# Even layer of a two-layer backbone: where the modulation's row sums stand among the first projection blocks, and how many buffers the heads' results have

## The chip, the cores and the metric

One core of a Trainium2 chip runs the whole kernel in one launch. The metric is the device time of that launch in microseconds, the median of several executions. A profile is one profiled execution; its times are counted from the start of its span.

## The reference, cut to what matters

```python
def adaln(cond, w, b):
    m = jax.nn.silu(cond) @ w + b
    return jnp.split(m, 3, axis=-1)              # shift, scale, gate

def even_layer(x, ctx, c, c_ctx, ...):           # x 512x2048, ctx 256x2048
    sh, sc, gt = adaln(c, ada_w, ada_b)
    csh, csc, cgt = adaln(c_ctx, ada_w, ada_b)
    h  = modulate(rms_norm(x, norm_g), sh, sc)
    hc = modulate(rms_norm(ctx, norm_g), csh, csc)
    kc_t, vc_t = split(hc @ w_in[:, K and V])
    au, av, ag, bq, bk, bv, bg = split(h @ w_in)
    q, k = diff_qk(bq, qnorm_g, cos, sin), diff_qk(bk, knorm_g, cos, sin)
    ...                                          # attention over latents and context,
    return x + gt * (y @ w_out)                  # gated mixing, output projection

def odd_layer(x, c, ...):                        # a convolution module with its own adaln
    sh, sc, gt = adaln(c, ada_w, ada_b)
    h = modulate(rms_norm(x, norm_g), sh, sc)
    return x + gt * (conv_module(h, ...) @ w_out)
```

`diff_qk` normalises each head's 64 values and rotates them by position (the latents only). All is fp32. What the change moves is a part of `adaln`: the products of silu(c) with the gate part of the even layer's modulation weights and with the three parts of the odd layer's, four vectors of 2048.

## The kernel before

**Arithmetic.** Every fp32 matrix product is made of three: each operand is split into a high part (a cast to float32r) and a low part (the rest), and TensorE (PE) multiplies high by high, low by high and high by low. `load_w` (L98) does this for a granule of weights, four k-tiles of 128x512: a DMA of 1 MB in SP's queue into a `raw` buffer (three of them, shared with the row loads below), the high cast on ACT (L103), the subtraction on VectorE (DVE, L104). There are two buffers for each half.

**Blocks.** `m_block` (L170) makes a block of 512 output columns: one PSUM tile for each 128 tokens, six with the context and four without, from a ring of six (tag "m" of `psA`), and four granules. In each granule PE goes through the token tiles, 12 matmuls for each; a call `hook(gi)` follows each granule in the program. A latent tile uses `hhi` and `hlo`, a context tile the two halves of `hc`.

**The order of the work around the change.** First come the shift and scale of the even layer, interleaved with the first K block (L376 to L419). There PE's and SP's order is written out by hand; it fills `k0ps`, the tiles mb_333 to mb_338. Its last two context k-tiles end it: `make_hc` (L363 to L371) has PE transpose ctx (L366), ACT scale it into `hcf` (L368), and DVE make `hc`, high (L109) and low (L112). Then follow, in the program: `k_done(k0ps)`, the first V block (L593, tiles mb_1441 to mb_1446), `v_done`, some small loads (`rows2` and four `dwr`, L597 to L616, and lam), the second K block, the second V block, two Q blocks (L637, four tiles each), and from there AV, U, the attention and the output projection. A list scheduler decides how the engines' instructions stand against each other, outside the part written by hand: by its own simulation of the times, with weights preferred (`high_priority`). The order on each engine is fixed before the run.

**A K or Q result.** `qk_post` (L532) takes each finished tile: ACT squares it (L534), DVE reduces it (L537) and scales (L193), POOL takes the power -1/2 (L194, `rs`), DVE makes `tn` = tile times `rs` (L541), the last to read the PSUM tile, so that the tile is free for the next block, then for a latent tile the rotation (L549 to L555), for a context tile one product (L557). PE transposes the result `rot` (L560), ACT casts the high part (`qkhi`, L111), DVE subtracts (`qklo`, L112), and both are written to DRAM (L565). `qkhi` and `qklo`, and `vhi` and `vlo` of `v_post`, share a ring with the tag "hl" of three buffers; a buffer is free when its write to DRAM has landed.

**The row sums.** The four vectors of the modulation above are made beside the blocks. `ada_jobs` (L447) lists 64 rows, 16 for each vector: row jt is 128 lines of the weight matrix, 128x2048, 1 MB. `ada_add` (L464, L466) multiplies it by a column of silu(c) and adds it to `acc` on DVE; after 16 rows a tail sums over the partitions and writes it out (`spread`, `columns`, `row`, in later calls). A call of `ada_step` adds first the row loaded ahead, then takes and adds n rows from the `raw` ring, and with a pool `w0` loads one more ahead into w0's single buffer. So `hook0` (L590) adds two rows a call, `hook` one, and no call of theirs goes across the end of a vector. Before, `hook0` stands behind all granules of V, K, V and of Q's first block, `hook` behind those of Q's second.

Of the kernel before, what the change touches and what calls it, by code (L numbers as in the profile page):

```python
# [11 lines left out]
F32 = mybir.dt.float32  # L12
F32R = mybir.dt.float32r
# [6 lines left out]
P = 128  # L20
D = 2048
KT = D // P
T = 512
# [12 lines left out]
C_U, C_AV, C_AG, C_Q, C_K, C_BV, C_BG = 0, 1024, 2048, 3072, 4096, 5120, 6144  # L36
# [9 lines left out]
def hybrid_layers_kernel(  # L46
# [10 lines left out]
    e_ada_w, e_w_in, e_w_out = e_ada_w[0], e_w_in[0], e_w_out[0]  # L57
# [4 lines left out]
    def nm(s):  # L62
        uid[0] += 1
        return f"{s}_{uid[0]}"
# [187 lines left out]
    PE.transpose(tpz, rows1, ident[:96, :96])  # L252
    V.tensor_copy(g1, tpz)

    S = rp.tile([P, KT, 32], F32, name="S")
    V.memset(S, 0.0)
    th = tp.tile([P, 2 * KT], F32, tag="small", name="th")
    A.activation(th, g1[:, cC : cC + 2 * KT], AF.Tanh, scale=0.5)
# [59 lines left out]
    diag = tp.tile([P, T], F32, tag="a", name="diagx")  # L318
    rbz = zt()
    spread_cols(rbz, rsx, diag)  # L320
    rb = tp.tile([P, T], F32, tag="hl", bufs=3, name="rb")
    V.tensor_copy(rb, rbz)

    def load_ctx():
# [150 lines left out]
    def ada_step(zalloc, n=1, pool=None):  # L475
        if ada_tail:
            f = ada_tail.pop(0)
            f(zalloc)
            if f.__name__ == "spread":
                return  # L480
        done = False
        if ada_state["ahead"]:
            done = ada_add(ada_state["ahead"])
            ada_state["ahead"] = None
        for _ in range(n):
            if done or not (job := ada_take()):
                return
            done = ada_add(job)
        if pool and not done:
            ada_state["ahead"] = ada_take(pool)  # L490
# [41 lines left out]
    def qk_post(ps, which, tt, half, tok0, dst, rope):  # L532
        sq = tp.tile([P, 512], F32, tag="a", name=nm("sq"))
        A.activation(sq, ps, AF.Square)  # L534
        ms = tp.tile([P, 8], F32, tag="ms", bufs=4, name=nm("ms"))
        rs = tp.tile([P, 8], F32, tag="rs", bufs=4, name=nm("rs"))
        V.reduce_sum(ms, sq.rearrange("p (g d) -> p g d", d=DH), axis=AX.X)  # L537
        rstd_cols(rs, ms, 1.0 / DH, ms)
        tn = tp.tile([P, 512], F32, tag="b", name=nm("tn"))
        g3 = lambda a: a.rearrange("p (g d) -> p g d", d=DH)  # L540
        V.tensor_tensor(g3(tn), g3(ps), rs.unsqueeze(2).broadcast_to([P, 8, DH]), op=ALU.mult)  # L541
        r = tp.tile([P, 512], F32, tag="c", name=nm("rot"))
        if rope:
            CG, SG = CGs[which], SGs[which]
            g5 = lambda a: a.rearrange("p (g a b d) -> p (g a) b d", g=8, a=2, b=2)
            s5 = SG[:, tt, :].rearrange("p (a b d) -> p a b d", a=2, b=2)
            t5 = lambda a, b: a.rearrange("p (g a b d) -> p g a b d", g=8, a=2, b=2)[:, :, :, b, :]
            for b in range(2):
                V.tensor_tensor(  # L549
                    t5(r, b), t5(tn, 1 - b),  # L550
                    s5[:, :, b, :].unsqueeze(1).broadcast_to([P, 8, 2, 16]),
                    op=ALU.mult,
                )
            V.tensor_tensor(g3(tn), g3(tn), CG[:, tt, :].unsqueeze(1).broadcast_to([P, 8, DH]), op=ALU.mult)
            V.tensor_tensor(r, r, tn, op=ALU.add)  # L555
        else:
            V.tensor_tensor(g3(r), g3(tn), gains[which].unsqueeze(1).broadcast_to([P, 8, DH]), op=ALU.mult)  # L557
        z = zt()
        for i in range(4):
            PE.transpose(z[:, i * P : (i + 1) * P], r[:, i * P : (i + 1) * P], ident)  # L560
        hi = tp.tile([P, 4, P], F32R, tag="hl", bufs=3, name=nm("qkhi"))
        lo = tp.tile([P, 4, P], F32R, tag="hl", bufs=3, name=nm("qklo"))
        split(hi, lo, z.rearrange("p (a b) -> p a b", b=P))
        for s, tl in ((0, hi), (1, lo)):
            SP.dma_start(  # L565
                dst[4 * half : 4 * half + 4, s, :, tok0 : tok0 + P].rearrange("h p t -> p h t"), tl.bitcast(F32)
            )

    def v_post(ps, half, tok0):
        hi = tp.tile([P, 4, P], F32R, tag="hl", bufs=3, name=nm("vhi"))  # L570
        lo = tp.tile([P, 4, P], F32R, tag="hl", bufs=3, name=nm("vlo"))
        split(hi, lo, ps.rearrange("p (a b) -> p a b", b=P))
        for s, tl in ((0, hi), (1, lo)):
            SP.dma_start(
                v_s[4 * half : 4 * half + 4, s, tok0 : tok0 + P, :].rearrange("h t d -> t h d"), tl.bitcast(F32)
            )
# [5 lines left out]
    def v_done(ps, half):  # L582
        for b in range(NT + NTC):
            v_post(ps[b], half, b * P)
# [3 lines left out]
            qk_post(ps[b], 0, b, half, b * P, q_s, True)  # L588

    hook0 = lambda gi: ada_step(zt, 1, w0)  # L590
    hook, hook2 = (lambda gi, n=n: ada_step(zt, n) for n in (1, 2))
    k_done(k0ps, 0)
    ps = m_block(e_w_in, C_BV, both(), psA, "m", hook0)  # L593
    v_done(ps, 0)


# [36 lines left out]
    k_done(ps, 1)  # L633
    ps = m_block(e_w_in, C_BV + 512, both(), psA, "m", hook0)
    v_done(ps, 1)
    for hb in range(2):
        ps = m_block(e_w_in, C_Q + 512 * hb, lat(), psA, "m", hook if hb else hook0)  # L637
        q_done(ps, hb)
    p12a.close()

# [638 lines left out]
```

## Time and profile before

| | |
|---|---|
| median of 3 runs | 1862.2 us (1861.59 to 1863.13) |
| the profiled execution's own time | 1862.0 us |
| its span | 1860.2 us |
| mean granted TensorE clock | 0.994 |
| busy of the span: PE, PEld, DVE, ACT, POOL | 97%, 79%, 60%, 30%, 24% |
| DMA | 327.34 MB, mean 176 GB/s |

PE is TensorE's matmul, PEld its weight load, SP the engine whose queue issues the DMAs. A row of a timeline gives the start in us, the duration of one instruction (or of a run of equal ones together), engine, line, operation, what it writes and reads, and in brackets the idle time before it with what ended it. Matmuls are pipelined, so that a matmul's duration of 0.39 us is longer than the step to the next. A row of a window gives start and end, the length, then for PE, PEld, DVE, ACT and POOL the busy time with the count of instructions, PE's granted clock (1.00 is full), the mean busy share of the 16 DMA engines, and GB/s. In names the numbers are dropped by the profile; lists of the order keep them.

### The profile page before, as it was taken

How to read it: one execution, taken by the hardware profiler on the slowest of the kernel's cores; microseconds unless marked ns; L12 is line 12 of the kernel's file. 1: busy time of each engine (PE TensorE's matmuls, PEld its weight loads, DVE VectorE, ACT ScalarE, POOL GpSimd, SP SyncE). 2: the span in 40 equal slices, each digit the busy share in tenths (PEclk: the TensorE clock that was granted, in tenths of full speed). 3: DMA queues.
4: the chain of work that ended last, by engine and by line, in shares of the span. 5: the costliest groups of instructions: out<-in, count | busy, mean ns of one | idle time of the engine just before them, and what ended most of it. 6: DMA issues, size and time to landing. Idle time of an engine off the chain costs nothing.

```text
span 1860.2 us, 21958 instructions
## 1 busy us (share of the span) xinstructions
PE 1808.0 (97%) x8767; PEld 1478.0 (79%) x8767; DVE 1122.4 (60%) x1571; ACT 560.5 (30%) x747; POOL 451.2 (24%) x173
## 2 busy tenths in 40 slices
PE   5998999999999989999999999999999999999998
PEld 2556878888888878888888889888888888888887
DVE  4439545377656336667674555249999999765111
ACT  3322112122323134444442225322222222464120
POOL 0002002002000032323220002234544544444332
PEclk9998999999999999999999999999999999999999
DMA  9997763496667485565757663232233223224441
GB/s 321 359 347 243 246 201 115 145 348 227 207 246 248 150 224 165 159 193 149 213 184 241 237 223 106 76 106 91 91 108 97 91 93 112 91 91 141 145 159 53
DMA packets 208487, 327.34 MB, mean 176 GB/s; under 512 B 10249, under 2 KB 116610, under 8 KB 200194
## 3 DMA queue, kind: packets, MB, share of 16 engines
q1 hardware_dynamic: 208386, 325.94, 54.5%
q8 instruction: 69, 1.13, 0.3%
q14 instruction: 32, 0.26, 0.0%
HBM read 292.33 MB, written 33.58 MB: 175 GB/s over the span
## 4 chain that ended last, share of the span: by engine, by line
PE 81%; DMA 9%; DVE 4%; issue 3%; POOL 1%; ACT 1%; SPq 1%; DVEq 0%; ACTq 0%; POOLq 0%
PE tg L67 30%; PE mb L67 19%; PE m L67 14%; PE fm L67 8%; DMA raw<-in_o_ada_w_dram 2%; PE S L67 2%; PE z L305 2%; DMA raw<-in_e_ada_w_dram 2%; PE oT L67 2%; DVE wlo L104 1%; DVE acc L466 1%; DMA v_s<-vhi 1%; PE t L875 1%; DMA x<-in_x_dram 1%; DMA kk<-k_s 1%
## 5 line engine op out<-in xcount | busy, mean ns | idle before, releaser
L104 POOL TENSOR_TENSOR wlo<-raw,whi 128x2048 fp32r<-128x2048 f32 x80 | 369.5, 4619 | 636.7 <-ACT whi L103 629.3
L103 ACT CAST whi<-raw 128x2048 fp32r<-128x2048 f32 x136 | 259.9, 1911 | 686.9 <-PE tg L67 212.5
L1144 DVE SCALAR_TENSOR_TENSOR z<-y,dwc,z 128x512 f32<-128x512 f32 x480 | 319.2, 744 | 0.1
L67 PE MATMUL tg<-h2h,wlo 128*128 128x512 f32 x704 | 274.7, 390 | 0.0
L67 PE MATMUL tg<-h2l,whi 128*128 128x512 f32 x704 | 273.9, 389 | 0.0
L67 PE MATMUL tg<-h2h,whi 128*128 128x512 f32 x704 | 270.8, 389 | 0.0
L67 PE MATMUL mb<-wlo,hhi 128*128 128x512 f32 x512 | 202.7, 396 | 1.5 <-DVE wlo L104 1.5
L104 DVE TENSOR_TENSOR wlo<-raw,whi 128x2048 fp32r<-128x2048 f32 x56 | 128.2, 2289 | 125.4 <-ACT whi L103 125.3
L67 PE MATMUL mb<-whi,hhi 128*128 128x512 f32 x512 | 203.0, 399 | 0.1
L67 PE MATMUL mb<-whi,hlo 128*128 128x512 f32 x512 | 201.7, 394 | 0.0
L466 DVE SCALAR_TENSOR_TENSOR acc<-raw,silu_c,acc 128x2048 f32<-128x2048 f32 x60 | 141.0, 2350 | 87.6 <-DMA raw<-in_o_ada_w_dram 69.6
L67 PEld LDWEIGHTS tg<-h2h,wlo 128*128 128x128 f32 x704 | 132.1, 188 | 27.9 <-issue 0.5
L67 PEld LDWEIGHTS tg<-h2l,whi 128*128 128x128 f32 x704 | 132.1, 188 | 27.9 <-issue 0.5
L67 PEld LDWEIGHTS tg<-h2h,whi 128*128 128x128 f32 x704 | 132.1, 188 | 27.3
L194 POOL TENSOR_TENSOR rs<-ms,mhalf 128x8 f32<-128x8 f32 x20 | 42.6, 2137 | 378.2 <-DVE ms L193 378.2
L67 PEld LDWEIGHTS mb<-whi,hhi 128*128 128x128 f32 x512 | 97.4, 190 | 33.8 <-issue 13.1
L67 PEld LDWEIGHTS mb<-wlo,hhi 128*128 128x128 f32 x512 | 97.4, 190 | 20.9 <-DVE wlo L104 1.7
L67 PEld LDWEIGHTS mb<-whi,hlo 128*128 128x128 f32 x512 | 97.5, 190 | 20.6
L67 PE MATMUL fm<-hhi,whi 128*128 128x512 f32 x256 | 106.7, 417 | 0.3 <-DVE mx L703 0.3
L67 PE MATMUL fm<-hlo,whi 128*128 128x512 f32 x256 | 101.1, 395 | 0.0
L67 PE MATMUL fm<-hhi,wlo 128*128 128x512 f32 x256 | 100.7, 393 | 0.0
L67 PE MATMUL m<-wlo,y2h 128*128 128x512 f32 x256 | 99.6, 389 | 0.0
(260 smaller groups left out, 3001.1 us busy)
## 6 DMA issues: line engine op xcount, KB each, us to landing
raw<-in_e_w_in_dram SPq DMA_DIRECT2D x56, 1024.0 KB, 6.0
raw<-in_o_ada_w_dram SPq DMA_DIRECT2D x48, 1024.0 KB, 5.1
raw<-in_o_w_in_dram SPq DMA_DIRECT2D x48, 1024.0 KB, 5.1
raw<-in_e_ada_w_dram SPq DMA_DIRECT2D x64, 512.0 KB, 8.4
raw<-in_e_ada_w_dram SPq DMA_DIRECT2D x16, 1024.0 KB, 6.9
raw<-in_e_w_out_dram SPq DMA_DIRECT2D x16, 1024.0 KB, 5.1
raw<-in_o_w_out_dram SPq DMA_DIRECT2D x16, 1024.0 KB, 5.0
qq<-q_s SPq DMA_DIRECT2D x16, 512.0 KB, 14.0
```

Source lines behind the costliest of these rows:

```text
L67: return PE.matmul(o, l, r, start=start, stop=stop)
L103: A.copy(hi, raw)
L104: (lo_eng or V).tensor_tensor(lo, raw, hi.bitcast(F32), op=ALU.subtract)
L194: G.tensor_tensor(dst, tmp, mhalf[:, 0:1].broadcast_to([P, n]), op=ALU.pow)
L305: PE.matmul(ada_ps[j][32 * g : 32 * g + 32, 0 : 2 * nc_], S[:, kt, :], raw[:, i, :], start=(kt < 4), stop=(kt >= KT - 4), skip_group_check ...
L466: V.scalar_tensor_tensor(ada_state["acc"], raw, sc_[:, jt : jt + 1], ada_state["acc"], op0=ALU.mult, op1=ALU.add)
L875: PE.transpose(z[:, k * P : (k + 1) * P], e[:, (k0 + k) * P : (k0 + k + 1) * P], ident)
L1144: V.scalar_tensor_tensor(zi if t == TAPS - 1 else z, y2[:, t : t + T], w(t), z, op0=ALU.mult, op1=ALU.add)
```

## The change

Three things. The tile `S` (128x16x32), which only the first modulation products read, moves from a pool of its own to the ring "hl", and the ring has four buffers instead of three; the memory in all stays the same, since `S` no longer needs its own. The first V block's first granule has no `ada_step` behind it. And Q's eight granules have `hook0` seven times and then `hook`, instead of four times each.

```diff
-    S = rp.tile([P, KT, 32], F32, name="S")
+    S = tp.tile([P, KT, 32], F32, tag="hl", bufs=4, name="S")
...
-        hi = tp.tile([P, 4, P], F32R, tag="hl", bufs=3, name=nm("qkhi"))
-        lo = tp.tile([P, 4, P], F32R, tag="hl", bufs=3, name=nm("qklo"))
+        hi = tp.tile([P, 4, P], F32R, tag="hl", bufs=4, name=nm("qkhi"))
+        lo = tp.tile([P, 4, P], F32R, tag="hl", bufs=4, name=nm("qklo"))
...
+    def hook_v0(gi):
+        if gi:
+            ada_step(zt, 1, w0)
+
...
-    ps = m_block(e_w_in, C_BV, both(), psA, "m", hook0)
+    ps = m_block(e_w_in, C_BV, both(), psA, "m", hook_v0)
     v_done(ps, 0)
...
+    q_steps = [hook0] * 7 + [hook]
+    hook_q = lambda gi: q_steps.pop(0)(gi)
     for hb in range(2):
-        ps = m_block(e_w_in, C_Q + 512 * hb, lat(), psA, "m", hook if hb else hook0)
+        ps = m_block(e_w_in, C_Q + 512 * hb, lat(), psA, "m", hook_q)
         q_done(ps, hb)
```

(`rb`, `vhi` and `vlo` get the fourth buffer in the same way.) Rows added of the first vector after each of V's four granules were 1, 3, 5, 7; now they are 0, 1, 3, 5. The first vector's tail comes at the second V block, one granule later than before. After Q's second block both have loaded 32 rows; the order of the instructions from the AV block on is the same, and so is the order up to about 142 us of the profile.

On PE, at the end of the first K block (mb_337 and mb_338 are its context tiles, hc_1250 and hc_1258 the last two context k-tiles, mb_1441 is the first tile of the V block), before:

```order
L366 MATMUL z_1253<-ident,cx_444 128x128
L366 MATMUL z_1253<-ident,cx_460 128x128
L67 MATMUL mb_337<-whi_1014,hc_1250 128x512
L67 MATMUL mb_337<-wlo_1015,hc_1250 128x512
L67 MATMUL mb_1441<-whi_1449,hhi_393 128x512
L67 MATMUL mb_1441<-wlo_1450,hhi_393 128x512
L67 MATMUL mb_1441<-whi_1449,hlo_394 128x512
L67 MATMUL mb_1441<-whi_1449,hhi_399 128x512
```

and after:

```order
L366 MATMUL z_1253<-ident,cx_444 128x128
L366 MATMUL z_1253<-ident,cx_460 128x128
L67 MATMUL mb_337<-whi_1014,hc_1250 128x512
L67 MATMUL mb_337<-wlo_1015,hc_1250 128x512
L67 MATMUL mb_337<-whi_1014,hc_1250 128x512
L67 MATMUL mb_338<-whi_1014,hc_1250 128x512
L67 MATMUL mb_338<-wlo_1015,hc_1250 128x512
L67 MATMUL mb_338<-whi_1014,hc_1250 128x512
L67 MATMUL mb_337<-whi_1014,hc_1258 128x512
L67 MATMUL mb_337<-wlo_1015,hc_1258 128x512
L67 MATMUL mb_337<-whi_1014,hc_1258 128x512
L67 MATMUL mb_338<-whi_1014,hc_1258 128x512
```

Before, V's first 12 matmuls (mb_1441) stand behind two of the K block's last 12 and ahead of the other ten. Now all 12 of K stand first, and V behind them.

On DVE, at the same place (ms are the reductions of K's results, acc the row sums, hc the halves of the context tile, tn_1304 the first K result, which frees mb_333), before:

```order
L537 TENSOR_REDUCE ms_1324<-sq_1322 128x8
L193 TENSOR_SCALAR ms_1299<-ms_1299 128x8
L466 SCALAR_TENSOR_TENSOR acc_1527<-raw_1610,silu_c,acc_1527 128x2048
L193 TENSOR_SCALAR ms_1324<-ms_1324 128x8
L537 TENSOR_REDUCE ms_1349<-sq_1347 128x8
L537 TENSOR_REDUCE ms_1374<-sq_1372 128x8
L109 CAST hc_1250<-hcf_1248 128x256
L109 CAST hc_1258<-hcf_1256 128x256
L541 TENSOR_TENSOR tn_1304<-mb_333,rs_1300 128x512
```

and after:

```order
L537 TENSOR_REDUCE ms_1324<-sq_1322 128x8
L109 CAST hc_1250<-hcf_1248 128x256
L193 TENSOR_SCALAR ms_1299<-ms_1299 128x8
L109 CAST hc_1258<-hcf_1256 128x256
L193 TENSOR_SCALAR ms_1324<-ms_1324 128x8
L537 TENSOR_REDUCE ms_1349<-sq_1347 128x8
L112 TENSOR_TENSOR hc_1250<-hcf_1248,hc_1250 128x256
L112 TENSOR_TENSOR hc_1258<-hcf_1256,hc_1258 128x256
L537 TENSOR_REDUCE ms_1374<-sq_1372 128x8
L466 SCALAR_TENSOR_TENSOR acc_1605<-raw_1688,silu_c,acc_1605 128x2048
L193 TENSOR_SCALAR ms_1349<-ms_1349 128x8
L541 TENSOR_TENSOR tn_1304<-mb_333,rs_1300 128x512
```

The casts of hc move ahead of two reductions and of the row sum, the low parts (L112) ahead of the fourth reduction; a row sum that stood between the first two scales is gone from there, and one stands behind the fourth reduction, ahead of tn_1304. On ACT, `hcf` moves ahead of the third and the fourth square.

On DVE, in Q's second block, from the weights of its third granule to those of its fourth, before:

```order
L104 TENSOR_TENSOR wlo_3194<-raw_3191,whi_3193 128x2048
L549 TENSOR_TENSOR rot_3056<-tn_3054,SG_1285 128x16x16 x2
L112 TENSOR_TENSOR qklo_3017<-z_3011,qkhi_3016 128x512
L554 TENSOR_TENSOR tn_3054<-tn_3054,CG_1284 128x512
L555 TENSOR_TENSOR rot_3056<-rot_3056,tn_3054 128x512
L104 TENSOR_TENSOR wlo_3251<-raw_3248,whi_3250 128x2048
```

and after:

```order
L104 TENSOR_TENSOR wlo_3193<-raw_3190,whi_3192 128x2048
L112 TENSOR_TENSOR qklo_2986<-z_2980,qkhi_2985 128x512
L466 SCALAR_TENSOR_TENSOR acc_2677<-raw_3188,silu_c,acc_2677 128x2048
L541 TENSOR_TENSOR tn_3048<-mb_2720,rs_3044 128x512
L554 TENSOR_TENSOR tn_3023<-tn_3023,CG_1284 128x512
L112 TENSOR_TENSOR qklo_3011<-z_3005,qkhi_3010 128x512
L466 SCALAR_TENSOR_TENSOR acc_2677<-raw_3245,silu_c,acc_2677 128x2048
L549 TENSOR_TENSOR rot_3050<-tn_3048,SG_1285 128x16x16 x2
L555 TENSOR_TENSOR rot_3025<-rot_3025,tn_3023 128x512
L104 TENSOR_TENSOR wlo_3253<-raw_3250,whi_3252 128x2048
```

Before, no row sum stands between these two sets of weights; now there are two.

More of the change, by code (lines that the diff above doesn't have):

```diff
@@ L320, in hybrid_layers_kernel @@
     spread_cols(rbz, rsx, diag)
-    rb = tp.tile([P, T], F32, tag="hl", bufs=3, name="rb")
+    rb = tp.tile([P, T], F32, tag="hl", bufs=4, name="rb")
     V.tensor_copy(rb, rbz)
@@ L569, in v_post @@
     def v_post(ps, half, tok0):
-        hi = tp.tile([P, 4, P], F32R, tag="hl", bufs=3, name=nm("vhi"))
-        lo = tp.tile([P, 4, P], F32R, tag="hl", bufs=3, name=nm("vlo"))
+        hi = tp.tile([P, 4, P], F32R, tag="hl", bufs=4, name=nm("vhi"))
+        lo = tp.tile([P, 4, P], F32R, tag="hl", bufs=4, name=nm("vlo"))
         split(hi, lo, ps.rearrange("p (a b) -> p a b", b=P))
```

## Prediction

> **What bounds the kernel now.** I read the page first, then the waits of TensorE, the windows over the stretch that the change touches, and its timelines. The profiled execution took 1862.0 us: a span of 1860.2 and 1.8 around it; the median of the three runs is 1862.2, and they lie 1.5 apart. A measurement of this kernel can tell about 0.2%, 3.7 us, from no change.
>
> The page's first lines, the DMA line for the second weight matrix of the modulation, and one window (its length, then busy time and instruction count of PE, PEld, DVE, ACT and POOL, PE's clock, DMA share, GB/s):
>
> ```profile
> span 1860.2 us, 21958 instructions
> PE 1808.0 (97%) x8767; PEld 1478.0 (79%) x8767; DVE 1122.4 (60%) x1571; ACT 560.5 (30%) x747; POOL 451.2 (24%) x173
> raw<-in_o_ada_w_dram SPq DMA_DIRECT2D x48, 1024.0 KB, 5.1
> 255.00:640.00 385.00, 385.00 (x1771) 316.66 (x1771) 212.86 (x205) 96.92 (x102) 31.97 (x18) 1.00 0.60 205
> ```
>
> PE is the bound: 97% of the span, and without a gap from 255 to 640. So a microsecond is worth something only where PE stands or runs slowly. From 150 to 255 its waits are these (total, times, longest; one of 0.2 left out):
>
> ```profile
> PE mb L67 <- DVE hc L109: 3.4, 1, 3.4
> PE z L560 <- DVE rot L555: 2.3, 1, 2.3
> PE z L610 <- DMA dwr<-in_o_dw_w_dram: 1.7, 3, 0.8
> PE mb L67 <- DVE wlo L104: 1.5, 1, 1.5
> ```
>
> Three of the four are for DVE, at the seam where the first K block ends and the first V block begins. The seam on PE's timeline (start, duration), from the last context transposes to the first matmul of V's third granule:
>
> ```profile
> 152.52 0.60 PE L366 MATMUL z<-ident,cx 128*128 128x128 f32 x4
> 156.52 0.53 PE L67 MATMUL mb<-whi,hc 128*128 128x512 f32 x1 [3.40 <-DVE hc L109]
> ...
> 164.12 0.39 PE L67 MATMUL mb<-whi,hhi 128*128 128x512 f32 x1
> ...
> 166.61 0.39 PE L67 MATMUL mb<-whi,hlo 128*128 128x512 f32 x1
> ...
> 172.27 0.79 PE L67 MATMUL mb<-wlo,hhi 128*128 128x512 f32 x1 [1.48 <-DVE wlo L104]
> ...
> 204.18 0.39 PE L67 MATMUL mb<-whi,hhi 128*128 128x512 f32 x1
> ```
>
> From 164.12 to 166.61 lie 11 steps, 0.2267 us a matmul. The stretch from 153.12 (end of the transposes) to 204.18, all instructions first and PE's matmuls of L67 second:
>
> ```profile
> 153.12:204.18 51.06, 43.54 (x181) 34.84 (x181) 38.70 (x56) 9.59 (x14) 13.46 (x6) 0.90 0.74 235
> 153.12:204.18 51.06, 41.27 (x157) 0.90 0.74 235
> ```
>
> 157 matmuls at 0.2267 are 35.6; the other 24 instructions are six groups of four transposes, about 0.39 a group in a full pipe (my estimate, from 0.60 for a group with its tail of some 0.2), 2.35. That is 37.95 at full speed, so the stretch lost 13.1 of its 51.06. Waits are 3.40 + 2.27 + 1.48 + 0.24 = 7.4. The rest is mostly the clock:
>
> ```profile
> 51.67:55.09 3.42, 1.36 (x10) 0.51 (x11) 3.00 (x12) 1.52 (x2) 0.70 (x1) 1.00 1.10 351
> 55.09:58.50 3.41, 3.41 (x19) 1.92 (x18) 3.24 (x8) 0.00 (x0) 0.00 (x0) 1.00 1.10 355
> 154.07:157.49 3.42, 0.84 (x3) 0.41 (x3) 3.42 (x10) 0.20 (x1) 3.42 (x2) 1.00 0.98 350
> 157.49:160.90 3.41, 3.41 (x9) 2.67 (x10) 3.29 (x6) 0.00 (x0) 3.41 (x3) 0.53 0.53 207
> 167.73:171.14 3.41, 0.79 (x6) 0.42 (x4) 3.41 (x3) 0.90 (x2) 0.00 (x0) 1.00 1.08 365
> 171.14:174.55 3.41, 2.28 (x5) 1.82 (x6) 3.41 (x6) 0.27 (x1) 0.91 (x1) 0.53 0.90 276
> 174.55:177.97 3.42, 3.42 (x9) 2.64 (x8) 3.34 (x9) 0.00 (x0) 2.36 (x2) 0.50 1.00 331
> ```
>
> The clock falls to half in steps of 3.41 us, always in the window behind one in which PE was busy 23 to 25% of the time (167.73, 154.07); behind 40% (51.67) it stays whole. In the seam 3.41 us and 2.28 + 3.42 = 5.70 us of work ran at half: 1.7 + 2.85 = 4.55 lost. With the waits that makes 11.95; some 1.2 stay unexplained (pipe ends, missing records).
>
> The Trainium skill ("TensorE: Matmul & The Clock Gate", Part 1, "The HAM clock gate") has a free-running window of 3413 ns, which the trace bears out to the step. Its section "HAM oscillation" puts the danger at idle gaps over some 3.4 us; by that the gaps of 2.27 and 1.48 would have cost no clock, and the trace halved it behind them, so here the measurement decides.
>
> **The change, part by part.** *The missing row.* Before the seam, what DVE and ACT did was (start, duration):
>
> ```profile
> 151.30 1.36 DVE L537 TENSOR_REDUCE ms<-sq 128x8 f32<-128x512 f32 x2 [0.52 <-ACT sq L534]
> 152.65 2.35 DVE L466 SCALAR_TENSOR_TENSOR acc<-raw,silu_c,acc 128x2048 f32<-128x2048 f32 x1
> 156.19 0.48 DVE L109 CAST hc<-hcf 128x256 fp32r<-128x256 f32 x2
> 156.59 0.68 DVE L541 TENSOR_TENSOR tn<-mb,rs 128x512 f32<-128x512 f32 x1
> 157.33 0.75 DVE L112 TENSOR_TENSOR hc<-hcf,hc 128x256 fp32r<-128x256 f32 x2
> 169.94 2.28 DVE L104 TENSOR_TENSOR wlo<-raw,whi 128x2048 fp32r<-128x2048 f32 x1
> 150.67 2.69 ACT L534 ACTIVATE sq<-mb 128x512 f32<-128x512 f32 x4 [6.46 <-PE mb L67]
> 153.25 1.01 ACT L368 ACTIVATE hcf<-z,shc,Ac 128x256 f32<-128x256 f32 x2
> 164.32 1.92 ACT L103 CAST whi<-raw 128x2048 fp32r<-128x2048 f32 x1
> ```
>
> A row sum of 2.35 and two reductions stood ahead of the casts that PE waited for, and on ACT two squares ahead of hcf. In the new order hcf follows the second square, the casts follow the second reduction, no row sum is between, and PE finishes K before it begins V. PE's idle time, step by step:
>
> - Casts: hcf can start as the transposes end, about 153.0; half of 1.01 makes 153.5, a cast of 0.24 makes 153.8, and PE goes on at 153.87: 0.75 idle where 3.40 were.
> - Low part: two matmuls later PE needs the low part of hc, which in DVE's order stands behind the third reduction, and that behind the third square (ACT 154.0 to 154.6, since hcf now goes first). Reduction to 155.2, subtraction 0.37, PE at 155.66: 1.33 idle. This wait is new; all PE work behind it queues.
> - V's first PSUM tile: ten matmuls later, at 157.92, V wants the tile that the first K result occupies until its tn is made. In the new order tn stands behind the second low part, the fourth reduction and one row sum (2.27 until the next starts): 155.9 + 0.6 + 2.27 and the small scale, so 158.85 to 159.53, and PE at 159.65: 1.7 idle, new too. The powers on POOL, 5.34 for the first two (next fence), are ready in time for the first.
> - Second granule's low weights: its high cast stands on ACT behind the square of K's fifth tile, which PE, finishing K first, ends at about 157.2; so it can go at about 158.1, where 164.32 was; on DVE tn, a reduction, a row sum and the rotations come first, so 163.7 to 166.0, and PE is there at 165.5: 0.5 idle where 1.48 was.
> - First rotated transposes: operands at 169.8, PE at 171.0; the 2.27 are gone. The next two are covered by 1.2 only.
>
> Sum of the idle: 4.3. PE is then busy 49% of the worst window, if windows lie as before (157.49 to 160.90 holds the 1.7), above the 40% that kept the clock, so I take no half clock. The stretch is 37.95 + 4.3 = 42.25 instead of 51.06: 8.8 gained. Bounds: idle is at least 2.5 (0.75, low part 0.75, tile 1.0, no more), if squares and sum run a little earlier; and at most 6.5, if the tile takes the 3.40 of the old first wait and the weights 0.3 more.
>
> *The fourth buffer.* Rows of the next part, the chain's powers on POOL among them:
>
> ```profile
> 152.82 5.34 POOL rs L194 x2
> 193.09 0.69 DVE L112 TENSOR_TENSOR qklo<-z,qkhi 128x512 fp32r<-128x512 f32 x1 [2.77 <-DMA k_s<-qkhi]
> 198.79 0.69 DVE L112 TENSOR_TENSOR qklo<-z,qkhi 128x512 fp32r<-128x512 f32 x1 [3.50 <-DMA k_s<-qklo]
> 180.37 2.35 DVE L466 SCALAR_TENSOR_TENSOR acc<-raw,silu_c,acc 128x2048 f32<-128x2048 f32 x1 [2.47 <-DMA raw<-in_e_ada_w_dram]
> raw<-in_e_ada_w_dram SPq DMA_DIRECT2D x12, 1024.0 KB, 7.1
> 150.00:255.00 105.00, 95.82 (x413) 77.18 (x412) 68.57 (x82) 20.91 (x26) 13.75 (x6) 0.95 0.79 256
> ```
>
> With three buffers DVE stood 2.77 and 3.50 for a result's write to DRAM, and the third granule's weights came behind it: wlo ended only 1.5 before PE's 204.18. PE comes 8.8 earlier now; with three it would have waited up to the sum of the two, 6.3. The fourth buffer removes that: alone it is worth nothing, here it carries part of the 8.8. I book nothing for it; its bounds, 0 to a loss of 6.3 if it doesn't work, belong to a rival. The memory comes from a tile that is dead by then.
>
> *Row loads in SP's queue.* One row's load leaves the queue ahead of V's second granule and later ones shift. Gain on PE none by itself. The late row at 180.37 stood 2.47 for its load; should the one ahead of the second rotations do the same, the 1.2 of cover is eaten and up to 0.9 is lost; I take 0 and keep 0.9 for the range. The small loads (dwr, 1.7 of waits in three) now come to PE eight, eight and five matmuls later, 1.8 and 1.1 us, longer than the longest wait of 0.8: with SP's queue as it is I take 1.2 of the 1.7, bounds 0 and 1.7.
>
> *Rows moved to Q.* Q's second block now holds seven row sums instead of five, and two loads more:
>
> ```profile
> 419.30:464.70 45.40, 45.40 (x209) 37.57 (x208) 35.15 (x48) 12.16 (x12) 10.68 (x5) 1.00 0.70 232
> 371.74 2.35 DVE L466 SCALAR_TENSOR_TENSOR acc<-raw,silu_c,acc 128x2048 f32<-128x2048 f32 x1 [3.33 <-DMA raw<-in_o_ada_w_dram]
> ```
>
> DVE is idle for 10.25 of the block's 45.40; two sums take 4.7 and leave 5.55. A row is asked for one granule ahead, 48 matmuls or 10.9 us, and lands in 5.1. PE's weights stay ahead of it, so this costs 0; if the cover were gone, 4.7. Behind it the order is the same, PE-bound, and moves along.
>
> **Sum:** 8.8 + 1.2 = 10.0 off the profiled 1862.0 is 1852.0; off the median, 1852.2.
>
> **The rivals.** *The clock still halves* (chance 0.18). The first two idle pieces lie within one 3.4 us: 0.75 + 1.33 leave 39% busy if a window falls there, between the 25% that halved and the 40% that didn't. Its place before (154.07) cuts them apart, which speaks against; a late square or row speaks for. One window costs 1.7, two 3.4: 1853.9 to 1855.6.
>
> By the skill's gap rule no piece here comes near 3.4 us and this rival would have no chance; the trace has already gone against it.
>
> *The gain is given back* (0.10). Weights and rows land no earlier, and PE, 9 us ahead, waits for them before 255: 1862. The DMA share of 0.79 in 150 to 255 speaks for it. Against: 256 GB/s there and 350 in the window at 154.07, so these bytes need 77 of 105 us. A fourth buffer that is not free in time would give back 6.3 and lies between, 1858.5.
>
> *Slower* (0.08): Q's second block. If each of the seven sums stands for its row as the one at 371.74 does, 3.33 each, DVE is 23.3 behind; 5.55 are covered, 17.8 reach PE through the low weights queued behind the sums: 1870. It is slower than before by 3.7 from (5.55 + 10.0 + 3.7)/7 = 2.75 us a row. Against: the 5.1 of landing in 10.9.
>
> **How the numbers follow.** Forecast 0.64, 1852.2. Its own range: idle 2.5 to 6.5 and dwr 1.7 to 0 give a gain of 12.3 to 6.6, 1849.9 to 1855.6; 1.4 below for the runs' spread makes 1848.5. Above, the clock's case with the same spread reaches 1857. That range holds 0.64 and 0.18. Faster by over 0.2%: 0.82; within: 0.10; slower: 0.08.
>
> **What would show it.** Right: the first matmul of V's third granule near 195.4; waits there of about 0.75 and 1.3 for hc and 1.7 for tn; no wait for rot; the windows behind 154 at a clock of 1.00; no DMA wait ahead of qklo near 185; dwr under 0.8 in sum; no wait of PE from 400 to 460. Wrong: a half clock behind 154, a wait for wlo in the third granule or in Q, or one for rows before 255.

## The result, and the profile after

The changed kernel took 1854.18 us (median of 4 runs, 1850.40 to 1855.54) where the kernel before took 1862.66 (4 runs, 1861.59 to 1864.08): 8.5 us less where 10.0 were forecast. The ratio of the two on record is 0.9947 with a 95% interval of 0.9934 to 0.9959, which is 7.6 to 12.3 us; the two medians alone give 0.9954. The profiled execution took 1853.68, 1851.9 of it span.

Its page:

```profile
span 1851.9 us, 21931 instructions
PE 1805.9 (98%) x8767; PEld 1475.8 (80%) x8767; DVE 1122.3 (61%) x1571; ACT 559.8 (30%) x747; POOL 446.9 (24%) x173
```

PE's waits from 150 to 260 (total, times, longest):

```profile
PE mb L67 <- DVE ms L193: 1.4, 1, 1.4
PE mb L67 <- DVE hc L112: 0.9, 1, 0.9
PE mb L67 <- DVE hc L109: 0.8, 1, 0.8
```

The four old waits (3.4, 2.3, 1.7, 1.5) are gone or small, and three short ones stand in their place. The seam on PE's timeline, from the last transposes of ctx on; the last row holds the first matmul of V's third granule:

```profile
155.43 0.60 PE L366 MATMUL z<-ident,cx 128*128 128x128 f32 x4
156.85 0.50 PE L67 MATMUL mb<-whi,hc 128*128 128x512 f32 x1 [0.81 <-DVE hc L109]
157.19 0.39 PE L67 MATMUL mb<-wlo,hc 128*128 128x512 f32 x1
158.52 0.74 PE L67 MATMUL mb<-whi,hc 128*128 128x512 f32 x2 [0.94 <-DVE hc L112]
...
162.47 0.47 PE L67 MATMUL mb<-whi,hhi 128*128 128x512 f32 x1 [1.35 <-DVE ms L193]
...
198.41 0.84 PE L67 MATMUL mb<-whi,hhi 128*128 128x512 f32 x3
```

0.81 for the cast and 0.94 for the low part, then 1.35 for V's first PSUM tile. The last wait's releaser is named as the scale on DVE; what PE needed is tn ahead of it on the same engine. DVE's rows there:

```profile
159.31 2.34 DVE L466 SCALAR_TENSOR_TENSOR acc<-raw,silu_c,acc 128x2048 f32<-128x2048 f32 x1
161.57 0.17 DVE L193 TENSOR_SCALAR ms<-ms 128x8 f32<-128x8 f32 x1
161.64 0.69 DVE L541 TENSOR_TENSOR tn<-mb,rs 128x512 f32<-128x512 f32 x1
162.24 0.17 DVE L193 TENSOR_SCALAR ms<-ms 128x8 f32<-128x8 f32 x1
```

The row sum of 2.34 us stands ahead of tn, as the order said. The stretch as a window, and Q's second block (start and end, length, PE, PEld, DVE, ACT, POOL, clock, DMA share, GB/s):

```profile
156.03:198.41 42.38, 39.14 (x182) 31.65 (x182) 34.64 (x55) 10.09 (x15) 10.76 (x6) 1.00 0.69 221
...
411.40:456.80 45.40, 45.40 (x210) 37.53 (x209) 39.83 (x51) 12.01 (x13) 8.57 (x6) 1.00 0.81 272
```

The stretch takes 42.38 where it took 51.06; the clock is whole (1.00) throughout; and Q's block costs PE nothing, with DVE busy for 39.83 of 45.40. Where the 8.3 us of the two spans come from needs one more place, the attention's first matmul, of before and of after:

```profile
680.88 2.90 PE L67 MATMUL S<-kk,qq 128*128 128x256 f32 x8 [6.29 <-DMA kk<-k_s]
```

```profile
672.63 2.90 PE L67 MATMUL S<-kk,qq 128*128 128x256 f32 x8 [3.75 <-DMA qq<-q_s]
```

| part of the span | before | after | difference |
|---|---|---|---|
| start to the end of the last context transposes | 153.12 | 156.03 | +2.9 |
| from there to V's third granule | 51.06 | 42.38 | -8.7 |
| from there to PE's arrival at the attention | 470.41 | 470.47 | +0.1 |
| PE's wait there for kk or qq | 6.29 | 3.75 | -2.5 |
| the rest | 1179.3 | 1179.3 | 0.0 |

Two of these rows, +2.9 and -2.5, were in no term of the prediction. In the third, the waits for dwr (1.7) went, and two for low weights, 1.3 together with the longer of 1.1 in AV, came.

The attention's first wait costs more than its own length, because PE runs at half speed behind it. The first row below is the kernel before, over two windows of 3.41 us from the last microsecond of the wait on; the second is e10 (below), where that wait is gone, from its first attention matmul on:

```profile
679.93:686.76 6.83, 5.88 (x16) 4.85 (x17) 1.82 (x2) 1.04 (x1) 0.00 (x0) 0.50 1.06 208
```

```profile
676.16:682.99 6.83, 6.83 (x32) 5.65 (x33) 2.72 (x5) 3.16 (x5) 0.56 (x1) 1.00 1.08 245
```

PE gets through 16 instructions in its 5.88 us of the first and through 32 in its 6.83 us of the second. The changed kernel has the half speed here too, from 671.77 to 678.60, so that this loss does not show in the difference of the two.

### The profile page after: what moved, and what is told of

It is laid out like the page before. It is cut to its first block, busy times and chain, and to the rows that moved or that the text cites. A ratio compares the mean times of both kernels' runs of the same rounds, so it can differ in the third digit from the quotient of the medians.

```text
span 1851.9 us, 21931 instructions
## 1 busy us (share of the span) xinstructions
PE 1805.9 (98%) x8767; PEld 1475.8 (80%) x8767; DVE 1122.3 (61%) x1571; ACT 559.8 (30%) x747; POOL 446.9 (24%) x173
## 4 chain that ended last, share of the span: by engine, by line
PE 83%; DMA 8%; DVE 4%; issue 2%; ACT 1%; POOL 1%; SPq 1%; DVEq 0%; ACTq 0%; POOLq 0%
PE tg L67 31%; PE mb L67 20%; PE m L67 14%; PE fm L67 8%; DMA raw<-in_o_ada_w_dram 3%; PE S L67 2%; PE oT L67 2%; PE z L305 2%; DVE wlo L104 2%; DVE acc L466 1%; DMA raw<-in_e_w_in_dram 1%; PE t L883 1%; DMA qq<-q_s 1%; DMA x_s<-x 1%; POOL wlo L104 1%
## 5 line engine op out<-in xcount | busy, mean ns | idle before, releaser
L194 POOL TENSOR_TENSOR rs<-ms,mhalf 128x8 f32<-128x8 f32 x20 | 35.5, 1784 | 377.8 <-DVE ms L193 377.8
```

What stands on the lines that cost most here:

```text
L194: G.tensor_tensor(dst, tmp, mhalf[:, 0:1].broadcast_to([P, n]), op=ALU.pow)
```

## The experiments

Theory A is the prediction's: the order of DVE's and ACT's work at the seam makes the gain. Its rivals are that the fourth buffer does, that the load taken out of SP's queue does, or that fewer sums in V do; theory C came up on the way. The table gives, of each profiled execution, the end of the context transposes, the time from there to the 157th projection matmul behind them (the first of V's third granule), PE's wait for kk or qq at the attention's start, the time from PE's arrival there until a hundred PE instructions have started (wait and half speed included; which instructions these are is the same in all kernels), and the median of all runs. The times are taken before rounding, so that the 42.38 above is 42.37 here. The kernel before, run beside them, had medians of 1863.95 to 1864.58.

| kernel | transposes end | stretch | wait at attention | first hundred there | median us | ratio to before (95%) |
|---|---|---|---|---|---|---|
| before | 153.12 | 51.06 | 6.3 | 29.2 | 1862.66 | |
| changed | 156.03 | 42.37 | 3.7 | 26.7 | 1854.18 | 0.9947 (0.9934 to 0.9959) |
| e1 changed, again | 154.86 | 42.32 | 4.5 | 26.9 | 1854.45 | 0.9945 (0.9927 to 0.9963) |
| e2 three buffers | 155.95 | 42.35 | 2.6 | 24.4 | 1853.29 | 0.9943 (0.9926 to 0.9960) |
| e3 four buffers alone | 153.62 | 50.42 | 5.2 | 27.9 | 1861.93 | 0.9987 (0.9974 to 0.9999) |
| e4 load, no sum | 154.87 | 44.69 | 0 | 20.2 | 1846.74 | 0.9902 (0.9884 to 0.9920) |
| e5 before, wait filled | 153.26 | 47.89 | 6.8 | 28.7 | 1856.07 | 0.9961 (0.9947 to 0.9976) |
| e6 two rows less | 153.55 | 45.87 | 4.8 | 26.5 | 1854.37 | 0.9951 (0.9936 to 0.9965) |
| e7 load on Q | 154.26 | 42.37 | 5.9 | 27.3 | 1855.01 | 0.9953 (0.9937 to 0.9968) |
| e8 one row | 153.73 | 43.86 | 6.6 | 28.8 | 1855.23 | 0.9953 (0.9935 to 0.9971) |
| e9 heads first | 153.96 | 42.33 | 1.6 | 21.8 | 1849.54 | 0.9915 (0.9893 to 0.9937) |
| e10 before, heads first | 154.15 | 50.82 | 0 | 20.8 | 1857.44 | 0.9960 (0.9945 to 0.9975) |
| e11 heads first, two loads | 153.80 | 42.34 | 0 | 20.1 | 1846.40 | 0.9899 (0.9880 to 0.9918) |
| e12 before, two loads | 155.51 | 51.26 | 0 | 20.1 | 1856.71 | 0.9959 (0.9945 to 0.9973) |

**e1, the changed kernel again.** No edit.

> The changed kernel itself, once more. In its first profile the transposes of the last context tiles ended at 156.03 where the kernel before has 153.12, because a load ahead of the change's place came late (one wait of 4.49 us for the modulation's weights); the stretch from there to V's third granule took 42.38 us, and PE waited 1.34 us for low weights in AV. Theory A (those 2.9 us and the 1.3 us are the chance of one execution): the start of the stretch lies elsewhere by some us, the stretch itself is within 0.5 us of 42.4, and the time lies between 1850 and 1856. Theory B (they belong to the change, since S now sits in another pool): the start is again near 156.

Measured: the stretch repeats to 0.05 us, the waits for low weights in AV are not there, the transposes end 1.2 earlier. Among all executions with the rows as before they end at 153.12, 153.26, 153.62, 154.15 and 155.51, with those of the change at 153.80 to 156.03 (e1, e7, e9 and e11 lie between). So theory A: the 2.9 us and the AV wait are one execution's chance.

**e2, the rows without the fourth buffer.**

```diff
-    S = tp.tile([P, KT, 32], F32, tag="hl", bufs=4, name="S")
+    S = rp.tile([P, KT, 32], F32, name="S")
...
-        hi = tp.tile([P, 4, P], F32R, tag="hl", bufs=4, name=nm("qkhi"))
+        hi = tp.tile([P, 4, P], F32R, tag="hl", bufs=3, name=nm("qkhi"))
```

(`rb`, `qklo`, `vhi` and `vlo` lose the fourth buffer in the same way.)

> The change of the rows alone: S back in its own pool and the ring hl with three buffers. Theory A (the row's absence at the seam makes the gain, the fourth buffer keeps a part of it): the seam to 171 is as in the changed kernel, then DVE or ACT stand for writes of k_s, and PE waits 2 to 6 us for the third granule's weights: 1856 to 1860. Rival (the fourth buffer makes the gain): near 1862. Second rival (the fourth buffer does nothing, since writes land in time): as the changed kernel, within 1 us.

Measured: 1853.29, as the changed kernel; the second rival's time holds and the expected loss of 2 to 6 us did not come. The reason is in ACT's order: the third granule's high cast, which before stood behind the last two qkhi and so behind their waits for the writes of k_s, now stands ahead of them. ACT in e2:

```profile
190.60 0.59 ACT L111 CAST qkhi<-z 128x512 fp32r<-128x512 f32 x1 [3.77 <-DMA k_s<-qklo]
191.09 0.20 ACT L633 ACTIVATE le<-ls 128x2 f32<-128x2 f32 x1
192.14 1.91 ACT L103 CAST whi<-raw 128x2048 fp32r<-128x2048 f32 x1 [0.84 <-PE mb L67]
```

One write still held a qkhi ahead of the cast, for 3.77 us, but the cast had to wait 0.84 us longer than that for PE, which still read the buffer it needs. In the changed kernel, with four buffers, the same cast starts at 192.26, released by PE too.

The execution held something else. Two windows of e2, cut at where its clock changes:

```profile
156.01:159.42 3.41, 1.72 (x6) 1.15 (x7) 2.82 (x9) 1.80 (x4) 2.55 (x2) 1.00 0.79 324
159.42:162.83 3.41, 3.27 (x8) 2.13 (x8) 3.41 (x6) 1.14 (x2) 1.94 (x2) 0.50 0.09 14
```

Here the clock did halve, for exactly 3.41 us, the prediction's second case. It cost nothing: K's last matmuls ran at half speed into the time in which PE would have stood for V's tile, and that wait is missing from e2's list. The stretch is 42.35 all the same.

**e3, the fourth buffer alone.** The same tiles edited in the kernel before, rows untouched.

> The fourth buffer alone, rows as before. Theory A: DVE's waits of 2.77 and 3.50 us for k_s go, PE's waits of 3.40, 2.27 and 1.48 stay, and the time is that of before within 1 us. Rival (the fourth buffer makes the gain): 1853 to 1856.

Measured: 1861.93, a ratio of 0.9987 (0.2 to 4.8 us less by the interval), and a stretch 0.6 shorter. DVE's waits for k_s did not go, as had been expected; in e3 they are 2.89 and 1.54 us where before has 2.77 and 3.50. Whether the 0.6 us are the buffer's is not shown: e10 and e12, with three buffers and the rows as before, differ by 0.4 between themselves. In the changed order the buffer is worth nothing that the runs show (e2). The three waits of the seam stay:

```profile
PE mb L67 <- DVE hc L109: 3.4, 1, 3.4
PE z L560 <- DVE rot L555: 2.3, 1, 2.3
PE mb L67 <- DVE wlo L104: 1.5, 1, 1.5
```

**e4, the load without the sum.**

```diff
         if gi:
             ada_step(zt, 1, w0)
+        else:
+            ada_state["ahead"] = ada_take(w0)
```

> As the changed kernel, but V's first granule is followed by the load of a row into w0's buffer, without a sum; later granules add two each. Here DVE's order has a row sum between the second and the third reduction, and the casts of hc behind the third; PE still finishes K first. Theory A (what counts is where the sum stands on DVE against the casts): the wait for the casts is about 2.8 us, the one for the low part about 0.8, the one for V's tile small, and one window's clock may halve: 1 to 3 us slower than the changed kernel. Rival (what counts is that a row's load left SP's queue ahead of V's weights): near the time before, 1860 or more. Second rival (the sums' places are indifferent once PE finishes K first): as the changed kernel within 0.5 us.

Measured at the seam: the wait for the casts is 2.8 as expected, two windows at half clock are behind it, and the stretch is 44.69, 2.4 longer than the changed kernel's in e1. The wait of PE from 150 to 200, and after it three windows of e4, cut where its clock changes:

```profile
PE mb L67 <- DVE hc L109: 2.8, 1, 2.8
```

```profile
153.55:156.96 3.41, 1.32 (x8) 0.88 (x6) 3.41 (x6) 2.25 (x5) 0.12 (x1) 1.00 0.56 235
156.96:160.38 3.42, 2.71 (x6) 1.73 (x7) 3.42 (x10) 0.00 (x0) 3.42 (x2) 0.50 0.79 254
160.38:163.79 3.41, 3.41 (x10) 2.65 (x9) 3.41 (x5) 0.84 (x2) 3.41 (x2) 0.50 0.32 71
```

A load ahead of V's weights did not bring back the time before, so SP's queue at the seam is not the cause. But the whole time is 1846.74, 7.7 less than e1, though the seam is worse. PE has no wait at the attention's start there. What differs there is one place in SP's queue, which the counting of rows has shifted: a weight load of 1 MB stands behind the loads of the first two heads' kk and qq instead of ahead of them. SP's timeline (start, duration), the changed kernel first and e4 second:

```profile
655.20 0.38 SPq L95 DMA_DIRECT2D raw<-in_e_w_in_dram  x1
657.84 1.32 SPq L831 DMA_DIRECT2D kk<-k_s  x2
659.20 1.86 SPq L834 DMA_DIRECT2D qq<-q_s  x2
```

```profile
658.44 1.32 SPq L833 DMA_DIRECT2D kk<-k_s  x2
659.81 1.27 SPq L836 DMA_DIRECT2D qq<-q_s  x2
...
669.50 0.54 SPq L95 DMA_DIRECT2D raw<-in_e_w_in_dram  x1
```

That is theory C: those 7 us were won 470 us behind the seam. The profiles bear out its size: the first hundred PE instructions at the attention take 20.2 us in e4 and 26.9 in e1. e9 to e12 test it.

**e5, the kernel before with its wait filled.**

```diff
         z = zt()
+        if which and half == 0 and tt in (1,):
+            for _ in range(8):
+                mm(z, hm[0][0][:, 0:P], hm[0][0], True, True)
         for i in range(4):
```

> The kernel before, with eight more matmuls of a finished operand on PE, written to the tile of the second rotated result and overwritten there by its transposes. They stand between the first and the second group of rotated transposes, where PE waits 2.27 us, and take 1.8 us. Theory A (the clock halves behind a window in which PE was busy 25% or less): the window of that wait is now 65 to 75% busy, the next two windows keep a clock of 1.00 where they had 0.53 and 0.50, and PE reaches the third rotated transposes up to 2.8 us earlier; what is left at the end is less, 0.5 to 2.8 us, since DVE's results come no earlier. Rival (the waits as such halve the clock, or the clock is no cause of time): clock 0.5 as before, time as before or 0.5 slower.

Measured: in e5, the window of 3.41 us that holds the wait, the next two (cut on from where its clock changed last, at 161.38), and the row in which both kernels wait for the second granule's low weights:

```profile
168.21:171.62 3.41, 2.33 (x12) 1.45 (x10) 3.41 (x3) 1.04 (x2) 0.00 (x0) 1.00 1.11 356
171.62:175.04 3.42, 2.62 (x11) 2.17 (x12) 3.42 (x7) 0.00 (x0) 1.26 (x1) 1.00 0.90 236
175.04:178.45 3.41, 3.41 (x16) 2.82 (x15) 3.00 (x8) 0.00 (x0) 2.01 (x2) 1.00 1.04 403
...
172.41 0.50 PE L67 MATMUL mb<-wlo,hhi 128*128 128x512 f32 x1 [1.55 <-DVE wlo L104]
```

The window is 68% busy, as theory A said, and the two behind it have a clock of 1.00 where before ran at half speed from 171.35 to 178.18. Up to the row above both kernels take the same, 19.15 us from the end of the transposes (172.41 here, 172.27 before). The stretch is 3.2 shorter, and all of it lies behind that row, where before worked 5.9 us at half speed, 2.95 lost. So it is shown that idle time on PE halved the clock behind it, that a few extra matmuls keep it whole, and that the clock makes nearly all of what the stretch gained. The whole time is 0.39% (0.24% to 0.53%) under that of before, 8.2 us between the medians. Of this the stretch has 3.2. PE's 1.7 of waits for dwr are gone too, which is not the clock: the scheduler put the first transpose of dwr elsewhere (at 202.6, before at 236.9). Where the rest comes from is open.

**e6, two rows less.**

```diff
-        if gi:
+        if gi > 1:
             ada_step(zt, 1, w0)
...
-    q_steps = [hook0] * 7 + [hook]
+    q_steps = [hook0] * 8
```

> As the changed kernel, but with no row behind V's second granule either (all of Q's granules take two then). DVE's order here has the first row's product between the reductions, the casts behind the fourth reduction, one row sum ahead of the first K result, and PE has V's first matmuls between K's last ones again. Theory A (the order at the seam makes the gain, not the number of sums in V): waits of about 2.3 us for the casts and 2 to 3 us for V's tile, with a half clock behind them: 2 to 5 us slower than the changed kernel. Rival (fewer sums in V are what makes it faster): 1 to 3 us faster than the changed kernel.

Measured: the waits of PE in e6 at the seam,

```profile
PE mb L67 <- DVE ms L193: 2.4, 1, 2.4
PE mb L67 <- DVE hc L109: 2.3, 1, 2.3
```

as theory A said, with two windows at half clock behind them (157.85 to 164.68), and a stretch of 45.87, 3.5 longer with even fewer sums in V. So it is the order, not the number. The time of the whole, 1854.37, does not show the 3.5 us: medians of six runs that lie 5 us apart, with the attention's wait between 2.6 and 6.8, are too coarse for it. For the seam the stretch decides, and for the time I can say only that it is not faster.

**e7, more work for DVE in Q's second block.**

```diff
+    def hook_q(gi):
+        if len(q_steps) <= 4:
+            for _ in range(2):
+                V.tensor_scalar(ada_state["acc"], ada_state["acc"], 1.0, None, op0=ALU.mult)
+        q_steps.pop(0)(gi)
```

> The changed kernel with two products of the row sum's accumulator by 1.0 (128x2048) ahead of the rows behind each granule of Q's second block: 1.28 us each, 10.2 us more work for DVE there, no more loads. The trace before left DVE idle for 10.25 us of that block, 4.7 of them taken by the change. Theory A: 5.55 us of cover, so PE waits up to 4.7 us there or in AV: 2 to 5 us slower than the changed kernel. Rival (the weights go ahead of all sums in DVE's order, so the sums cost nothing): as the changed kernel within 0.7 us.

Measured: 1855.01, no wait of PE in the block; Q's second block in e7:

```profile
409.50:454.90 45.40, 45.40 (x209) 37.59 (x208) 43.97 (x51) 12.07 (x12) 11.36 (x5) 1.00 0.83 273
```

DVE is busy 43.97 of 45.40 and PE never stands. Two of the eight added products run ahead of this window, at 400.1 and 403.5, and the weights' subtractions come between the sums in time. So the rival's time holds, though not its order (the weights do not all go ahead of the sums), and the cover is larger than 5.55 us.

**e8, one row behind V's second granule.**

```diff
-            ada_step(zt, 1, w0)
+            ada_step(zt, 1, None if gi == 1 else w0)
...
-    q_steps = [hook0] * 7 + [hook]
+    q_steps = [hook0] * 8
```

> As the changed kernel, but V's second granule adds a row without a load ahead (one instead of two), and all of Q's granules take two. In DVE's order the casts stand behind the fourth reduction and the first K result comes ahead of all row sums but the first. Theory A: the wait for the casts grows from 0.8 to about 1.2 us, the waits of 0.9 and 1.35 us for the low part and V's tile shrink to under 0.5 together; the second granule's low weights come later, and give back up to 2 us: as the changed kernel within 1.5 us, either way. Rival (the sum ahead of the first K result was the last thing that held the seam): 1.3 us or more faster.

Measured: PE's waits in e8 from 150 to 200:

```profile
PE mb L67 <- DVE wlo L104: 2.4, 1, 2.4
PE mb L67 <- DVE hc L109: 1.3, 1, 1.3
```

The wait for V's tile went, the one for the second granule's low weights came in its place, with a window at half clock behind it (166.02 to 169.44), and the stretch is 1.5 longer. Theory A; the sum ahead of tn is not a last obstacle, only the first of several of the same size.

**e9, the changed kernel with the heads' loads first.**

```diff
+            if (n, gi) == (2, 0):
+                with tc.issue_after(kq_dma[1].ins):
+                    return load_w(*args)
...
-            SP.dma_start(qq[ds_].bitcast(F32), q_s[h].rearrange("s (m d) t -> d (s m) t", d=DH))
+            kq_dma[h] = SP.dma_start(qq[ds_].bitcast(F32), q_s[h].rearrange("s (m d) t -> d (s m) t", d=DH))
```

> The changed kernel, and one weight load of 1 MB at the attention's start (the third pair of columns that fills PE there) put in SP's queue behind the loads of the first two heads' K and Q instead of ahead of them; that is the order that e4_load_no_sum had by chance. In the changed kernel PE stood 3.7 to 6.6 us for kk or qq there, in e4 not at all. Theory C (e4's 7 us beyond the changed kernel came from that place, not from the seam, where its stretch of 44.2 us is 1.8 longer): PE's wait for kk and qq is under 1 us, and the time is 3 to 7 us under the changed kernel's 1854.4: 1847.5 to 1851.5. Rival (e4 is faster because V's sums stand elsewhere, and the attention's start only follows): the wait moves to the weights, and the time stays within 1.5 us of 1854.4.

Measured: 1849.54, 4.9 under e1, though the runs overlap (1845.08 to 1852.44 against 1849.63 to 1857.69); PE's wait for qq is 1.6 us where under 1 was expected. No half speed follows it, and the first hundred PE instructions there take 21.8 us, 5.1 less than in e1. Theory C, with a rest.

**e10, the same swap in the kernel before.**

> The kernel before with the same single swap in SP's queue, no other edit: rows and buffers as before. Theory C: the wait of 6.3 us for kk goes, and 4 to 7 us with it: 1856 to 1860 where before has 1863 to 1864. Rival: as before within 1.5 us.

Measured: 1857.44, 6.5 under the runs of before beside it (1863.95; 4.7 to 10.3 by the interval), PE's wait of 6.3 gone, with 0.7 for ACT in its place, and the half speed behind it gone too. The swap is worth at least as much without the change under study.

**e11, two weight loads put behind.** As e9, with the second pair's second half, `(1, 1)`, behind the first head's qq, `kq_dma[0]`; the next load then falls behind the second head's.

> The changed kernel with two weight loads put behind: the second pair's second half behind the first head's K, Q and V, the third pair's first half behind the second head's. Theory C with bandwidth as the cause (kk and qq wait for the bytes queued ahead of them): no wait for kk and qq, as e9 within 1 us, or up to 3 us slower if the fill's weights are now late. Rival (only the load just ahead matters): as e9 within 0.5 us.

Measured: 1846.40, no wait for kk or qq at all; 17.6 us under the runs of before beside it (1863.95), the lowest median here. It is 3.1 under e9, which neither theory had said (the same within 1 us or slower, the same within 0.5 us). PE's wait is 4.5 in e1, 1.6 in e9 and 0 in e11, so both loads seem to count; these are single executions, and with one load put behind e10 had no wait for kk or qq either.

**e12, the same two loads in the kernel before.**

> The kernel before with the same two weight loads put behind as in e11, rows and buffers as before. It differs from e11 by the change under study alone, and the runs of e11 lay only 1.5 us apart (1845.1 to 1846.6, median 1846.4), so the pair shows the change's worth without the attention's start. Theory A (8.7 us at the seam, 1.2 to 1.7 from the small loads, no loss in Q): 1855.5 to 1857.5, its runs about as close together. Rival (a part of the changed kernel's 8.5 us was the shorter wait at the attention's start, 6.3 against 3.7): 1853 to 1854.5.

Measured: 1856.71, though its runs are not as close together (1853.77 to 1860.15). Beside e11 the change under study is worth 10.3 us between the medians, with the attention's wait at zero on both sides: theory A. The two were measured on different chips; by their ratios to the runs of before beside each, the change is worth 0.6%, some 11 us. Their stretches differ by 8.9.

## Why the prediction was right, and where it was not

The forecast was 1852.2, from 1848.5 to 1857.0; measured were 1854.18. The mechanism was right in its main place: the stretch was forecast at 42.25 and took 42.32 to 42.37 in all six executions with the changed order (changed, e1, e2, e7, e9, e11), and the two kernels without the attention's wait differ by 10.3 where the sum said 10.0. V's third granule began at 198.41, not near 195.4 as forecast, but the 2.9 us of the late start make that difference.

- *The idle time, term by term.* The profile lists 0.81, 0.94 and 1.35, 3.1 in sum, where the prediction has 4.3, but the two count differently. The prediction starts a wait when the next matmul would have begun, 0.23 us behind the last one's start; the profile starts it at the last one's end, 0.39 behind its start. Counted from the rows in the prediction's way, the casts cost 0.82 (forecast 0.75), the low part 1.22 (1.33), V's tile 1.68 (1.7) and the second granule's weights, in two long steps (168.26 to 168.78 to 169.12), 0.4 (0.5). That is 4.1 of 4.3, every term within 0.12.
- *The clock.* No window of the profiled execution halved. That is partly luck, as e2 shows: there a window of the same seam fell so that PE was busy for half of it, and the next one halved. The prediction priced that at 1.7 us; it cost nothing, since the next wait took it up. That price was wrong for this place: half speed costs only where PE has something left to be late for. The readings of 25, 23 and 40% busy were off too, because those windows were cut 0.2 us early (the clock of 0.53 in them shows it). Cut where the clock changes they are 31, 18 and 46% (last section). And "always" did not fit the prediction's own last row: the window at 174.55 ran at half speed behind one that was 67% busy.
- *The fourth buffer.* The prediction said that it carries a part of the gain, up to 6.3 us. It doesn't (e2). The step that failed is that the writes of k_s would hold the third granule's weights in the new order too; ACT's order had changed there as well, and that part of it I had not read.
- *The range.* The upper idle time of 6.5 comes to 6.3 from the terms that are named for it, and the 0.9 kept for a late row is in neither bound. The measured time lies far from both.
- *Rows in Q.* No cost, as forecast; the cover is larger than the 5.55 us given for it (e7). *Small loads.* 1.2 of 1.7 forecast; 1.7 went in the profile, 1.2 in e1.
- *"Behind it the order is the same, PE-bound, and moves along."* This failed. The wait at the attention's start did not move along: it was 6.3 in the profile before and 2.6 to 6.8 over the kernels whose SP queue is the same there. What makes it vary is open. In the two profiles it added 2.5 us to the gain, as the late start took 2.9 from it. Whether such differences made 8.5 of the 10.0 is not shown; 10.0 lies inside the interval of 7.6 to 12.3.

## What to carry to other kernels

When one change is timed by the whole, time a stretch too: from the last instruction that both kernels share to the first that both share again. Here the stretch repeated to 0.05 us while whole runs of one kernel mostly lay 5 to 8 us apart, and e4's whole time would have praised a seam that was worse. When moving work on one engine, read the new order of all engines around each term; the buffer's term fell because ACT's order had moved too. And look at what is queued ahead of a stage's first loads: one weight load of 1 MB ahead of kk and qq cost 4.9 us in the changed kernel and 6.5 in the one before, more than half of what the seam was worth. A part of that is the half speed behind the wait: the first hundred instructions at the attention took 29.2 us in the kernel before and 20.1 without a wait, 9.1 for a wait of 6.3.

## What the runs showed of the hardware

The clock halves for whole windows of 3.41 us. Windows of the kernel before, cut where its clock changes (the first three numbers are start and end, length, and PE's busy time; PE's clock is the third from the end):

```profile
51.88:55.30 3.42, 1.57 (x11) 0.68 (x12) 3.00 (x12) 1.52 (x2) 0.70 (x1) 1.00 1.10 351
154.28:157.70 3.42, 1.05 (x3) 0.60 (x4) 3.42 (x11) 0.00 (x0) 3.42 (x2) 1.00 0.94 335
157.70:161.11 3.41, 3.41 (x9) 2.65 (x8) 3.29 (x6) 0.00 (x0) 3.41 (x3) 0.50 0.49 192
167.94:171.35 3.41, 0.63 (x4) 0.42 (x4) 3.41 (x3) 1.10 (x2) 0.00 (x0) 1.00 1.06 358
171.35:174.76 3.41, 2.49 (x6) 2.01 (x7) 3.41 (x7) 0.06 (x1) 1.12 (x1) 0.50 0.96 289
174.76:178.18 3.42, 3.42 (x10) 2.65 (x9) 3.13 (x8) 0.00 (x0) 2.15 (x2) 0.50 0.95 325
```

Behind 31% and 18% busy the clock halved, behind 46% it stayed whole. Cut in this way, the fourteen profiles agree from where their records of the clock begin (28 to 31 us) to 1800 us. All 34 windows at full clock in which PE was busy for less than 43% were followed by half speed, and of some seven thousand with more than 51% none was. Between the two, 5 of 15 were, e2's window at 156.01 with 50% among them; what decides there is open. A halved window passed half speed on to the next one when PE was busy for 81% of it or less (17 windows), as in the row at 171.35 with 73%, and full speed from 84% on (39 windows). So the waits ahead of 171.35 cost two windows. Where the windows lie differs from one execution to the next (edges at 157.70 in before, at 159.42 in e2), so that the same kernel may or may not lose a window.

The Trainium skill ("TensorE: Matmul & The Clock Gate", section "HAM oscillation") warns of idle gaps over some 3.4 us; in e2 only gaps of 0.81 and 0.94 us lay ahead of the halved window, so here the trace shows that far shorter ones are enough.
